# One decoder layer with three token mixers and 32 experts on one core: taps ahead of the search, Silu later, squares summed by TensorE, sums of a block together

## The chip, the cores and the metric

The kernel runs on one core of a Trainium2 chip. The core has TensorE (PE in the profile; PEld is its weight load), VectorE (DVE), ScalarE (ACT), GpSimd (POOL) and SyncE (SP, which issues the DMAs), each with its own queue of instructions, worked off in order. The metric is the device time of one execution in microseconds (us). An execution that was profiled also leaves a trace; its span is the time from the first to the last instruction.

## The reference, cut to what matters

One layer for 512 tokens of width 1024, in float32:

```python
h = rms_norm(x, n1g) * (1 + sc1) + sh1
qm, km, vm, ca, cg, qd, kd, vd, qi, ki, wi = split(h @ w_in)
y_moba = moba_attention(qm, km, vm)            # 6 heads
y_conv = silu(layer_norm(causal_conv31(ca * sigmoid(cg))))   # 256 channels
y_dsa  = dsa_attention(qd, kd, vd, qi, ki, wi) # 6 heads, the 128 best keys per query
mix = concat([rms_norm(y_moba, mg), y_conv, rms_norm(y_dsa, dg)])
x = x + g1 * (mix @ w_out)
h2 = rms_norm(x, n2g) * (1 + sc2) + sh2
y = hier_moe(h2)   # best of 4 groups, best 2 of its 8 experts, each (silu(x@w1) * (x@w3)) @ w2
return rms_norm(x + g2 * y, final_g)
```

The convolution has 31 taps per channel; each is one multiply-add over 512 tokens. The 128 best keys are found by 16 rounds, each of which takes the 8 largest scores of a row and strikes them out.

## The kernel before, in words

**Order.** Every engine executes in the order in which the Python program emits. The program is one walk along TensorE's projection: `h @ w_in`, unit after unit, 8 steps (k) to a unit, three matmuls to a step (L458 to L460 for values, L463 to L465 for the rest, since operands are split in a high and a low part). Around it everything else is woven in by three devices. `step()` is called after each k step: it runs what was put off with `after(n, f)` once n steps are over, and on every third step (TEVERY = 3) it emits one entry of the list `taps`. `spent(us)` is told how long TensorE will be busy, times a rate, and spends that credit on three background lists `bg`, the first list that isn't empty first: `bg[0]` (the norm of group m and sums for the conditioning), `bg[1]` (the rounds of the top-score search on VectorE, L686 and L689) and `bg[2]` (VectorE's part of the convolution).

**Attention.** An item is a group (m or d), a query tile of 128 and a pair of heads: score matmuls (L628, L630), mask and row maximum on VectorE (L824), exponential on ScalarE (L826), scaling on VectorE (L834) and GpSimd (L838), then after some steps transposes (L845), copies to SBUF on ScalarE (L847), then the product with the values (L859) and a copy (L864). Items of group d need the mask of the search. After the third pair of a tile, `f3` squares the result on ScalarE (L868), GpSimd adds the three squares (L870, twice), and `f4` sums over the partitions by a matmul with ones (L878) into one column of the bank `pss[m]`. Once a group of tiles (GROUPS: tile 0 and tiles 1 to 3 for d) is done, the inverse root is taken on VectorE (L253 to L258), spread by L330, and applied.

**Convolution.** It has two halves of 128 channels. Of 31 taps per half, VectorE does a first one (L708) and 16 more (L712), ScalarE and GpSimd do 14 as a chain: ScalarE multiplies into a buffer of pool `g`, of which there are two (L723), and GpSimd adds (L724); the first of the 14 needs no addition (L719, L720). At the end of VectorE's list, `f2` emits whatever is left in `taps` at once and joins both sums (L729). Three steps (L5 = 3) after the second half, `conv_norm` has TensorE sum the channels (L743), VectorE subtract the mean (L750), ScalarE square, GpSimd add (L754), TensorE sum (L760), then the inverse root, its spreading (L330), the multiplication (L768) and Silu (L769).

**Tail.** After the projection (`tail[0] = 1`) the program goes on stepping until all twelve pieces of the mix are there, and the output projection (L1066 to L1068) and the last attention items of group d share TensorE.

**Experts.** 16 blocks of slots follow, the first alone and most others in pairs. A block does up-products with w1 (`up1`, 32 matmuls of 64x512, L1484), with w3 (`up3`), a transposition (L1508) and down-products (L1518); w1, w3 and w2 come by DMA from SyncE's queue. The result of a block is added to the tokens one block later by `added(nh)`, for each half nh of the columns: 8 matmuls (L1544) into four banks and four VectorE additions (L1536). In the odd blocks 1 to 13 `added(0)` is called in the middle of `up1` and `added(1)` behind it, each once.

Of the kernel before, what the change touches and what calls it, by code (L numbers as in the profile page):

```python
# [13 lines left out]
OP = mybir.AluOpType  # L14
PSUM = bass.MemoryType.PSUM

P = 128
T = 512
NT = 4
D = 1024  # L20
KD = 8
# [52 lines left out]
GROUPS = {"m": ((0, 1, 2, 3),), "d": ((0,), (1, 2, 3))}  # L74
# [8 lines left out]
def tile_hybrid_layer(  # L83
# [75 lines left out]
    def ps(shape, dt=F32):  # L159
        return mk(pp, shape, dt, "ps", 8)  # L160
# [60 lines left out]
    def col(name, j=0, n=1):  # L221
        i, r = rows[name]
        return pcol[i][:, r + j:r + j + n]
# [37 lines left out]
    def rsqrt(r, v, n, shape, apart=True):  # L261
        for f in rsqrt_ops(r, v, n, [P, r.shape[1]], apart):
            f()
# [263 lines left out]
    def spent(us):  # L527

        credit[0] = min(credit[0] + us * rate[0], CRED)
        while any(bg):  # L530
            b = [b for b in bg if b][0]
            if credit[0] < b[0][0]:
                break
            d, f = b.pop(0)
            credit[0] -= d
            f()
# [9 lines left out]
    def after(n, f):  # L546
        later.append([n, f])
# [192 lines left out]
    def conv_norm():  # L740
        pmean = ps([P, T])
        for j in range(2):
            PE.matmul(pmean, ones, cy[j], start=j == 0, stop=j == 1)  # L743
        spent(1.7)
        st = {}

        def f1():
            sq = []
            for j in range(2):
                V.scalar_tensor_tensor(cy[j], pmean, -1.0 / 256, cy[j], op0=OP.mult, op1=OP.add)  # L750
                q = ta([P, T])
                A.activation(q, cy[j], AF.Square)
                sq.append(q)
            G.tensor_tensor(sq[0], sq[0], sq[1], op=OP.add)  # L754
            after(L4, lambda: f2(sq[0]))

        def f2(sq):
            pv = ps([P, NT])
            for t_ in range(NT):
                PE.matmul(pv[:, t_:t_ + 1], sq[:, t_ * P:(t_ + 1) * P], ones[:, 0:1], start=True, stop=True)  # L760
            r = mk(sm, [P, NT], F32, "r4", 3)
            rsqrt(r, pv, 256, [P, NT])
            after(4, lambda: f3(r))

        def f3(r):
            p = spread(r).rearrange("p t q -> p (t q)")
            for j in range(2):
                V.tensor_tensor(cy[j], cy[j], p, op=OP.mult)  # L768
                A.activation(cu[j], cy[j], AF.Silu, bias=col("lb", j), scale=col("lg", j))  # L769
            for t_ in range(NT):  # L770
                for j in range(2):
                    mixed.append((t_, 3 + j, 1, cu[j][:, None, t_ * P:(t_ + 1) * P]))
        after(2, f1)
# [33 lines left out]
    def lag(i):  # L807

        return LT[i] if tail[0] else (L1, L2, L3, L4)[i]

    def att_item(m, qt, j):
# [39 lines left out]
        def f3():  # L851
            if (m, 6 + j) not in qkv:
                after(1, f3)
                return
            y = ps([P, P])
            for kt in range(qt + 1):
                for e in range(2):
                    hp = slice(64 * e, 64 * e + 64)
                    PE.matmul(y[hp], qkv[m, 6 + j][:, kt, hp], pT[e][:, kt * P:(kt + 1) * P],  # L859
                              start=kt == 0, stop=kt == qt)  # L860
            spent(0.22 * (qt + 1))
            if (m, qt) not in ym:
                ym[m, qt] = tq([P, 3, P])
            A.copy(ym[m, qt][:, j], y)  # L864
            npair[m, qt] = npair.get((m, qt), 0) + 1
            if npair[m, qt] == 3:
                sq = ta([P, 3, P])
                A.activation(sq, ym[m, qt], AF.Square)  # L868
                for i in (1, 2):
                    G.tensor_tensor(sq[:, 0], sq[:, 0], sq[:, i], op=OP.add)  # L870
                after(lag(3), lambda: f4(sq))

        def f4(sq):
            if m not in pss:
                pss[m] = ps([P, NT])
            pv = pss[m][:, qt:qt + 1]
            done.setdefault(m, set()).add(qt)
            PE.matmul(pv, sq[:, 0], ones[:, 0:1], start=True, stop=True)  # L878
            for g in GROUPS[m]:
                if qt in g and done[m].issuperset(g):  # L880
                    r = mk(sm, [P, NT], F32, "r4", 3)[:, :len(g)]
                    rsqrt(r, pss[m][:, g[0]:g[-1] + 1], 384, [P, NT])
                    after(L6 + 3 * (m == "m"), lambda r=r, g=g: f5(r, g))

        def f5(r, tiles):
# [432 lines left out]
    class Block:  # L1318
# [165 lines left out]
                    PE.matmul(self.pu[s, :], self.feature(k)[:, s], self.w[i][e][k // 4][:, k % 4, :],  # L1484
                              start=k == 0, stop=k == KD - 1)

        def up1(self, also=lambda: None):
            n = self.n
            self.up(0, range(4))
            also()  # L1490
            self.up(0, range(4, KD))
            self.hs = ta([P, T])
            A.activation(self.hs[:n], self.pu[:n], AF.Silu)  # L1493

# [207 lines left out]
    def added(nh):  # L1702

        if nh in old:
            blk, y = old.pop(nh)
            blk.combine(nh, y)
# [26 lines left out]
    for b in range(NB):  # L1733
# [5 lines left out]
            nxt = None if last else pair.blks[1 - b % 2]  # L1739

        fill = b > 0 and (b % 2 == 0 or last)
        cur.up1(lambda: None if fill else added(0))
        if b == 0:
            for t_ in range(2, NT):
                for i in range(2):
# [191 lines left out]
```

## Time and profile before

| | us |
|---|---|
| runs shown, three | 842.48, 844.48, 844.45 |
| their median | 844.45 |
| profiled execution | 841.79 |
| its span | 840.0 |
| TensorE busy in it | 803.2 |
| VectorE busy | 440.1 |
| ScalarE busy | 268.6 |
| GpSimd busy | 266.5 |

The profile is of one execution. Its page gives busy times, the trace behind it each instruction with its start, its duration and what ended the idle time before it. A granted clock of 1.00 means 2.4 GHz on TensorE, 0.50 means 1.2 GHz. Matmuls overlap by a part of their length, so a row's start plus its duration can lie behind the next row's start.

### The profile page before, as it was taken

The page shows a single profiled execution, that of the slowest core. Times are in us where ns is not written, and L with a number is a line of the kernel's source. Part 1 is how long each engine was busy: PE and PEld are TensorE (multiplying, and loading weights), DVE is VectorE, ACT ScalarE, POOL GpSimd, SP SyncE. Part 2 cuts the span into 40 slices and gives each one's busy share as a digit, 9 for nine tenths or more (in the row PEclk, how much of TensorE's full clock was granted, in tenths as well). Part 3 has the DMA queues.
Part 4 walks back from the last instruction along what each step waited for, and adds up shares of the span by engine and source line. Part 5 has one row for each costly group of instructions (what it writes and reads, how often), then busy time and mean ns, then how long its engine had stood idle before and what let it go on. Part 6 is the DMA issues. An engine that isn't in the chain of part 4 may idle for free.

```text
span 840.0 us, 12498 instructions
## 1 busy us (share of the span) xinstructions
PE 803.2 (96%) x4669; PEld 478.7 (57%) x4669; DVE 440.1 (52%) x1053; ACT 268.6 (32%) x577; POOL 266.5 (32%) x318
## 2 busy tenths in 40 slices
PE   6999999999989899999999999999999999999992
PEld 4888786677756678445446346436436445454442
DVE  4768888998767556673253152342333232332334
ACT  5277677646557333431101011101001001101024
POOL 0464876765403560605023031050050050050032
PEclk9999999999999999999999999999999999999997
DMA  9980574174215557789799999999999999999932
GB/s 346 337 194 1 201 234 158 48 265 150 65 64 183 244 204 305 288 339 393 283 420 419 420 420 418 420 419 419 418 421 418 421 418 420 419 419 394 375 120 103
DMA packets 75657, 252.00 MB, mean 300 GB/s; under 512 B 7511, under 2 KB 40385, under 8 KB 50506
## 3 DMA queue, kind: packets, MB, share of 16 engines
q1 hardware_dynamic: 75530, 251.15, 77.3%
q8 instruction: 38, 0.62, 0.3%
q14 instruction: 25, 0.20, 0.1%
q10 hardware_dynamic: 64, 0.02, 0.0%
HBM read 249.05 MB, written 2.10 MB: 299 GB/s over the span
## 4 chain that ended last, share of the span: by engine, by line
PE 84%; DVE 6%; ACT 3%; POOL 2%; DMA 1%; issue 1%; SPq 1%; ACTq 0%; POOLq 0%; DVEq 0%
PE ps L1484 26%; PE ps L1518 13%; PE ps L1544 7%; PE ps L1580 6%; PE ps L463 4%; PE ps L465 3%; PE ps L464 3%; PE ps L458 2%; PE ps L974 2%; DMA ad<-in_ada_w_dram 1%; PE ps L459 1%; PE ps L460 1%; PE ps L859 1%; PE ps L845 1%; PE ps L1508 1%
## 5 line engine op out<-in xcount | busy, mean ns | idle before, releaser
L1564 POOL TENSOR_SCALAR v<-c,sm 128x128 bf16<-128x128 f32 x112 | 65.0, 602 | 308.9 <-DVE sm L1595 308.9
L1484 PE MATMUL ps<-u,x 128*64 128x512 f32 x280 | 103.2, 594 | 0.0
L341 POOL TENSOR_TENSOR u<-r,u 128x512 fp32r<-128x512 f32 x55 | 73.6, 1345 | 54.2 <-ACT u L340 43.3
L1536 DVE TENSOR_TENSOR q<-ps,q 128x512 f32<-128x512 f32 x116 | 71.3, 681 | 32.3 <-PE ps L1544 32.3
L1501 DVE SCALAR_TENSOR_TENSOR a<-a,sm,ps 128x512 f32<-128x512 f32 x16 | 12.0, 747 | 133.9 <-PE ps L1484 97.8
L1484 PE MATMUL ps<-h,x 128*64 128x512 f32 x248 | 78.9, 594 | 0.0
L1484 PE MATMUL ps<-r,x 128*64 128x512 f32 x240 | 77.9, 593 | 0.0
L1518 PE MATMUL ps<-u,a 128*64 128x512 f32 x200 | 68.4, 595 | 0.0
L1529 ACT CAST a<-ps 128x512 fp32r<-128x512 f32 (+1 forms) x33 | 18.9, 573 | 133.0 <-DVE ps L1528 133.0
L1528 DVE TENSOR_TENSOR ps<-ps,q 128x512 f32<-128x512 f32 (+1 forms) x33 | 22.4, 678 | 68.0 <-PE ps L1518 68.0
L1544 PE MATMUL ps<-a,v 128*128 128x512 f32 (+1 forms) x132 | 53.9, 410 | 0.0
L463 PE MATMUL ps<-h,u 128*128 128x512 f32 x128 | 53.7, 419 | 0.0
L1484 PEld LDWEIGHTS ps<-u,x 128*64 128x64 f32 x280 | 31.5, 137 | 37.8 <-issue 35.6
L1518 PE MATMUL ps<-h,a 128*64 128x512 f32 (+1 forms) x144 | 50.5, 572 | 0.6 <-DVE g L1531 0.6
L1544 PE MATMUL ps<-g,v 128*128 128x512 f32 (+1 forms) x132 | 50.7, 386 | 0.0
L465 PE MATMUL ps<-h,u 128*128 128x512 f32 x128 | 50.5, 395 | 0.0
L464 PE MATMUL ps<-h,u 128*128 128x512 f32 x128 | 50.4, 394 | 0.0
L1484 PEld LDWEIGHTS ps<-r,x 128*64 128x64 f32 x240 | 24.2, 137 | 38.4 <-issue 35.5
L1588 ACT ACTIVATE x<-ps,c,c 128x256 f32<-128x256 f32 x28 | 14.3, 560 | 90.5 <-PE ps L1580 90.5
L1518 PE MATMUL ps<-r,a 128*64 128x512 f32 x120 | 43.0, 596 | 0.0
L1484 PEld LDWEIGHTS ps<-h,x 128*64 128x64 f32 x248 | 24.2, 137 | 31.1 <-issue 29.9
L1493 ACT ACTIVATE a<-ps 128x512 f32<-128x512 f32 x16 | 9.6, 598 | 99.7 <-PE ps L1484 91.4
(379 smaller groups left out, 1805.3 us busy)
## 6 DMA issues: line engine op xcount, KB each, us to landing
u<-in_expert_w_dram SPq DMA_DIRECT2D x60, 1024.0 KB
r<-in_expert_w_dram SPq DMA_DIRECT2D x48, 1024.0 KB
h<-in_expert_w_dram SPq DMA_DIRECT2D x46, 1024.0 KB
z<-in_expert_w_dram SPq DMA_DIRECT2D x24, 1024.0 KB
r<-in_ada_w_dram SPq DMA_DIRECT2D x16, 1024.0 KB
r<-in_w_in_dram SPq DMA_DIRECT2D x22, 512.0 KB
ad<-in_ada_w_dram SPq DMA_DIRECT2D x8, 1024.0 KB
h<-in_expert_w_dram SPq DMA_DIRECT2D x16, 256.0 KB
```

The lines of the kernel that those rows point to most:

```text
L341: eng.tensor_tensor(l, r, h.bitcast(F32), op=OP.subtract)
L463: PE.matmul(p, wh, h, start=k == 0, stop=False)
L464: PE.matmul(p, wh, l, start=False, stop=False)
L465: PE.matmul(p, wl, h, start=False, stop=k == KD - 1)
L1484: PE.matmul(self.pu[s, :], self.feature(k)[:, s], self.w[i][e][k // 4][:, k % 4, :], start=k == 0, stop=k == KD - 1)
L1518: PE.matmul(self.py[nh][s, cs], self.hT[:, k, s], self.second(e, k, nh)[:, cs], start=k == 0, stop=k == 3)
L1528: V.tensor_tensor(y, y, g2b[nh][:n, cs], op=OP.mult)
L1529: A.copy(yh, y)
L1536: V.tensor_tensor(xr[t_, nh], self.product(yy, t_), xr[t_, nh], op=OP.add)
L1544: PE.matmul(pc[:, cs] if held else pc, self.ot[:n, t_ * P:(t_ + 1) * P], yy[q][:n, cs], start=not held and q == 0, stop=last and q == 1)
L1564: ops.append(lambda o=b.choice(ch, t_), c_=c_[:, t_:t_ + 1]: eng.tensor_scalar(o, iota, c_, None, op0=OP.is_equal))
L1580: PE.matmul(p[:, kk], hb[q][t_][i][:, k * P:k * P + P], self.o[t_ // 2][:, t_ % 2], start=t_ == 0 and q == 0, stop=t_ == NT - 1 and q == 1)
```

## The change

1. `spent` serves the lists in the order `bg[0]`, `bg[2]`, `bg[1]`: VectorE's taps come before the rounds of the search.
2. The two Silus and the entries into `mixed` become `f4` of the convolution's norm, five steps after the multiplications.
3. In the tail (the last four tiles of group d) GpSimd's two additions of squares are left out; TensorE accumulates the three parts by three matmuls instead of one, and this comes one step sooner.
4. Each group of tiles has a bank of its own for its sums (`pss[m, gi]`).
5. `up1` isn't divided any more; `added(0)` and `added(1)` follow each other behind it in the odd blocks.

```diff
--- before.py
+++ after.py
@@ -528,7 +528,8 @@
 
         credit[0] = min(credit[0] + us * rate[0], CRED)
         while any(bg):
-            b = [b for b in bg if b][0]
+
+            b = [b for b in (bg[0], bg[2], bg[1]) if b][0]
             if credit[0] < b[0][0]:
                 break
             d, f = b.pop(0)
@@ -766,6 +767,11 @@
             p = spread(r).rearrange("p t q -> p (t q)")
             for j in range(2):
                 V.tensor_tensor(cy[j], cy[j], p, op=OP.mult)
+
+            after(5, f4)
+
+        def f4():
+            for j in range(2):
                 A.activation(cu[j], cy[j], AF.Silu, bias=col("lb", j), scale=col("lg", j))
             for t_ in range(NT):
                 for j in range(2):
@@ -866,20 +872,25 @@
             if npair[m, qt] == 3:
                 sq = ta([P, 3, P])
                 A.activation(sq, ym[m, qt], AF.Square)
-                for i in (1, 2):
-                    G.tensor_tensor(sq[:, 0], sq[:, 0], sq[:, i], op=OP.add)
-                after(lag(3), lambda: f4(sq))
-
-        def f4(sq):
-            if m not in pss:
-                pss[m] = ps([P, NT])
-            pv = pss[m][:, qt:qt + 1]
+
+                direct = bool(tail[0])
+                if not direct:
+                    for i in (1, 2):
+                        G.tensor_tensor(sq[:, 0], sq[:, 0], sq[:, i], op=OP.add)
+                after(lag(3) - direct, lambda: f4(sq, direct))
+
+        def f4(sq, direct):
+            gi = [qt in g for g in GROUPS[m]].index(True)
+            if (m, gi) not in pss:
+                pss[m, gi] = ps([P, NT])
+            pv = pss[m, gi][:, qt:qt + 1]
             done.setdefault(m, set()).add(qt)
-            PE.matmul(pv, sq[:, 0], ones[:, 0:1], start=True, stop=True)
-            for g in GROUPS[m]:
+            for i in range(3 if direct else 1):
+                PE.matmul(pv, sq[:, i], ones[:, 0:1], start=i == 0, stop=i == 2 * direct)
+            for gi, g in enumerate(GROUPS[m]):
                 if qt in g and done[m].issuperset(g):
                     r = mk(sm, [P, NT], F32, "r4", 3)[:, :len(g)]
-                    rsqrt(r, pss[m][:, g[0]:g[-1] + 1], 384, [P, NT])
+                    rsqrt(r, pss[m, gi][:, g[0]:g[-1] + 1], 384, [P, NT])
                     after(L6 + 3 * (m == "m"), lambda r=r, g=g: f5(r, g))
 
         def f5(r, tiles):
@@ -1484,11 +1495,9 @@
                     PE.matmul(self.pu[s, :], self.feature(k)[:, s], self.w[i][e][k // 4][:, k % 4, :],
                               start=k == 0, stop=k == KD - 1)
 
-        def up1(self, also=lambda: None):
+        def up1(self):
             n = self.n
-            self.up(0, range(4))
-            also()
-            self.up(0, range(4, KD))
+            self.up(0)
             self.hs = ta([P, T])
             A.activation(self.hs[:n], self.pu[:n], AF.Silu)
 
@@ -1739,7 +1748,7 @@
             nxt = None if last else pair.blks[1 - b % 2]
 
         fill = b > 0 and (b % 2 == 0 or last)
-        cur.up1(lambda: None if fill else added(0))
+        cur.up1()
         if b == 0:
             for t_ in range(2, NT):
                 for i in range(2):
```

Line numbers of the changed program are higher by 1 from L531 on, by 6 from the Silu on, by 9 to 11 from `f4(sq, direct)` on.

On GpSimd, the taps of the second half in the program before; q is the sum of a half, g the product of ScalarE's tap, u a split weight, v a softmax part.

```order
L724 TENSOR_TENSOR q_1336<-q_1336,g_1604 128x505
L838 TENSOR_TENSOR v_1576<-v_1576,sm_296_1564 128x128
L341 TENSOR_TENSOR u_1587<-r_1205,u_1587 128x512
L724 TENSOR_TENSOR q_1336<-q_1336,g_1677 128x504
L838 TENSOR_TENSOR v_1653<-v_1653,sm_316_1641 128x256
L341 TENSOR_TENSOR u_1715<-r_1415,u_1715 128x512
L724 TENSOR_TENSOR q_1336<-q_1336,g_1741 128x503
L724 TENSOR_TENSOR q_1336<-q_1336,g_1760 128x502
L838 TENSOR_TENSOR v_1730<-v_1730,sm_336_1718 128x384
L341 TENSOR_TENSOR u_1715<-r_1415,u_1715 128x512
L724 TENSOR_TENSOR q_1336<-q_1336,g_1818 128x501
```

The same engine after the change, from the addition that stands ahead of the last seven taps of the second half.

```order
L844 TENSOR_TENSOR v_1407<-v_1407,sm_237_1395 128x384
L341 TENSOR_TENSOR u_1415<-r_1185,u_1415 128x512
L725 TENSOR_TENSOR q_1203<-q_1203,g_1481 128x504
L725 TENSOR_TENSOR q_1203<-q_1203,g_1487 128x503
L725 TENSOR_TENSOR q_1203<-q_1203,g_1490 128x502
L725 TENSOR_TENSOR q_1203<-q_1203,g_1493 128x501
L725 TENSOR_TENSOR q_1203<-q_1203,g_1496 128x500
L725 TENSOR_TENSOR q_1203<-q_1203,g_1499 128x499
L725 TENSOR_TENSOR q_1203<-q_1203,g_1502 128x498
L844 TENSOR_TENSOR v_1464<-v_1464,sm_253_1452 128x512
L341 TENSOR_TENSOR u_1572<-r_1185,u_1572 128x512
```

Before, an addition for a weight or a softmax part stood between most taps; now the seven from 504 to 498 columns follow one another, and the 512-column softmax part and the next weight stand behind them.

On TensorE, the two matmuls that sum the channels for the convolution's mean (L743, of the two halves q) in the program before.

```order
L460 MATMUL ps_2532<-u_2172,h_107 128x256
L458 MATMUL ps_2532<-u_2172,h_105 128x256
L459 MATMUL ps_2532<-u_2172,h_105 128x256
L460 MATMUL ps_2532<-u_2172,h_107 128x256
L878 MATMUL ps_2347<-c_94,a_2403 128x1
L743 MATMUL ps_2606<-q_1913,c_94 128x512
L743 MATMUL ps_2606<-q_2235,c_94 128x512
L458 MATMUL ps_2532<-u_2172,h_105 128x256
L459 MATMUL ps_2532<-u_2172,h_105 128x256
```

The same two (now L744) after the change, with what stands around them.

```order
L629 MATMUL ps_1546<-q_1113,q_1111 128x256
L629 MATMUL ps_1547<-q_1114,q_1112 128x256
L631 MATMUL ps_1546<-q_1178,q_1111 128x256
L631 MATMUL ps_1547<-q_1178,q_1112 128x256
L463 MATMUL ps_1516<-h_105,u_1296 128x512
L464 MATMUL ps_1516<-h_107,u_1296 128x512
L465 MATMUL ps_1516<-h_105,u_1296 128x512
L744 MATMUL ps_1564<-q_924,c_94 128x512
L744 MATMUL ps_1564<-q_1195,c_94 128x512
L463 MATMUL ps_1516<-h_105,u_1296 128x512
L464 MATMUL ps_1516<-h_107,u_1296 128x512
```

Before, they stood among the projection of values, far behind the taps; now they stand in the projection of an earlier unit, one step behind the score matmuls of an attention item (L629, L631).

On TensorE, the middle of `up1` in an odd block before (L1484 up, L1544 sums of the block in front).

```order
L1484 MATMUL ps_4570<-r_4435,x_4254 64x512
L1484 MATMUL ps_4570<-u_4437,x_4254 64x512
L1544 MATMUL ps_4579<-a_4530,v_4354 128x512
L1544 MATMUL ps_4579<-g_4531,v_4354 128x512
L1544 MATMUL ps_4583<-a_4530,v_4354 128x512
L1544 MATMUL ps_4583<-g_4531,v_4354 128x512
L1544 MATMUL ps_4587<-a_4530,v_4354 128x512
L1544 MATMUL ps_4587<-g_4531,v_4354 128x512
L1544 MATMUL ps_4591<-a_4530,v_4354 128x512
L1544 MATMUL ps_4591<-g_4531,v_4354 128x512
L1484 MATMUL ps_4570<-u_4439,x_4254 64x512
L1484 MATMUL ps_4570<-u_4441,x_4254 64x512
```

The same block after the change, from the end of `up1`.

```order
L1495 MATMUL ps_4571<-u_4440,x_4255 64x512
L1495 MATMUL ps_4571<-u_4442,x_4255 64x512
L1495 MATMUL ps_4571<-u_4440,x_4255 64x512
L1495 MATMUL ps_4571<-u_4442,x_4255 64x512
L1553 MATMUL ps_4614<-a_4531,v_4355 128x512
L1553 MATMUL ps_4614<-g_4532,v_4355 128x512
L1553 MATMUL ps_4618<-a_4531,v_4355 128x512
L1553 MATMUL ps_4618<-g_4532,v_4355 128x512
```

The eight matmuls of `added(0)` went from the middle of the 32 up-products to behind them.

## Rows read from the trace of the kernel before

**Rows 1.** The page's first part: busy us, share of the span, instructions.

```profile
PE 803.2 (96%) x4669; PEld 478.7 (57%) x4669; DVE 440.1 (52%) x1053; ACT 268.6 (32%) x577; POOL 266.5 (32%) x318
```

**Rows 2.** Stretches: length, busy us by engine, granted clock, DMA share, GB/s.

```profile
120.00:140.00 20.00, 20.00 (x123) 13.36 (x121) 18.72 (x48) 14.47 (x38) 14.42 (x13) 1.00 0.52 159
247.00:290.00 43.00, 34.36 (x209) 23.56 (x208) 29.27 (x84) 25.96 (x65) 18.09 (x22) 0.96 0.55 208
252.70:256.05 3.35, 3.35 (x15) 2.80 (x13) 2.82 (x8) 2.21 (x5) 0.00 (x0) 0.50 0.52 149
444.58:504.40 59.82, 59.82 (x323) 29.07 (x324) 20.20 (x37) 6.76 (x12) 11.30 (x18) 1.00 1.01 420
804.00:808.00 4.00, 4.00 (x19) 2.06 (x15) 1.71 (x3) 0.00 (x0) 1.56 (x2) 1.00 0.39 125
```

**Rows 3.** TensorE's waits, 246 to 292 us: for whom, total, times, longest.

```profile
PE ps L859 <- ACT a L847: 5.5, 2, 4.2
PE ps L878 <- POOL a L870: 1.3, 2, 0.8
PE ps L330 <- DVE r L258: 1.0, 2, 0.8
PE ps L878 <- DVE ps L253: 0.9, 1, 0.9
```

**Rows 4.** The chain of waits from 425 to 510 us: start, duration, what.

```profile
433.49 3.43 PE ps L1484 x16
436.93 2.04 PE ps L1544 x8
438.96 3.58 PE ps L1484 x16
...
468.20 13.73 PE ps L1484 x64
...
484.45 1.85 PE ps L1544 x8
```

**Rows 5.** TensorE's timeline: start, duration, what; in brackets idle before, releaser.

```profile
133.59 0.39 PE L465 MATMUL ps<-h,u 128*128 128x512 f32 x1
...
220.27 1.96 PE L743 MATMUL ps<-q,c 128*128 128x512 f32 x4
...
237.58 0.94 PE L760 MATMUL ps<-c,a 128*128 128x1 f32 x8
...
251.66 1.37 PE L859 MATMUL ps<-a,q 128*64 128x128 f32 x12 [4.19 <-ACT a L847]
```

**Rows 6.** ScalarE's timeline from 246 to 251 us.

```profile
247.06 1.28 ACT L769 ACT_TABLE_LOAD   x1
249.42 1.52 ACT L769 ACTIVATE q<-q,m 128x512 f32<-128x512 f32 x2 [1.08 <-DVE q L768]
```

**Rows 7.** GpSimd's taps by line: count, ns of shortest, median, longest.

```profile
L724 POOL TENSOR_TENSOR q<-q,g x26: 1257/1276/1422, 80.8 to 168.1; 128x510 f32<-128x510 f32 x2, 128x509 f32<-128x509 f32 x2, 128x508 f32<-128x508 f32 x2, 128x507 f32<-128x507 f32 x2
```

**Rows 8.** GpSimd's timeline, three places between 130 and 194 us.

```profile
130.00 1.29 POOL L341 TENSOR_TENSOR u<-r,u 128x512 fp32r<-128x512 f32 x1 [1.27 <-ACT u L340]
131.26 1.27 POOL L724 TENSOR_TENSOR q<-q,g 128x507 f32<-128x507 f32 x1
134.84 1.27 POOL L838 TENSOR_TENSOR v<-v,sm 128x512 f32<-128x512 f32 x1 [2.32 <-DVE sm L830]
...
192.48 1.44 POOL L341 TENSOR_TENSOR u<-r,u 128x512 fp32r<-128x512 f32 x1 [1.76 <-ACT u L340]
```

**Rows 9.** VectorE's timeline, two places.

```profile
130.71 0.68 DVE L689 MATCH_REPLACE8 b<-sm,b 128x512 f32<-128x512 f32 x1
...
191.62 0.69 DVE L729 TENSOR_TENSOR q<-q,q 128x512 f32<-128x512 f32 x1
...
192.81 1.63 DVE L712 SCALAR_TENSOR_TENSOR q<-q,m,q 128x482 f32<-128x482 f32 x1
```

**Rows 10.** VectorE's taps by line: count, ns of shortest, median, longest.

```profile
L712 DVE SCALAR_TENSOR_TENSOR q<-q,m,q x32: 719/772/1819, 168.8 to 218.0; 128x482 f32<-128x482 f32 x2, 128x483 f32<-128x483 f32 x2, 128x484 f32<-128x484 f32 x2, 128x485 f32<-128x485 f32 x2
```

## The prediction

> **What bounds the kernel now.** I read the busy times first. TensorE is busy 803.2 of 840.0 us [rows 1], so the time can only move where TensorE idles or where its own matmuls get shorter or more. Next, by stretches [rows 2]: between 120 and 140 us TensorE is busy throughout, and VectorE beside it 18.72 of 20 us, with GpSimd at 14.42; between 247 and 290 us TensorE works 34.36 of 43 us, which leaves 8.64 idle; in a pair of expert blocks (444.58 to 504.40) it has no gap at all. A fifth row shows the granted clock at 0.50 from 252.70 to 256.05, that is at 1.2 GHz. So there are three stages with different laws: attention and projection, where TensorE is full but VectorE nearly so; the tail, where TensorE waits; and the experts, where only the length of the matmuls counts. The waits of the tail name whom TensorE waits for: 5.5 us for ScalarE's copies, 1.3 for GpSimd, 1.0 and 0.9 for VectorE [rows 3].
>
> The profiled execution took 841.79 us (span 840.0 and 1.79 around it); the median of the runs shown is 844.45, so 2.66 above it. I sum against the profiled execution and put the difference onto 844.45.
>
> **Both sums of the block in front together.** In an odd block, TensorE now goes from 16 up-products to 8 products of the earlier block, back to 16, and again to 8. The chain shows it: 3.43, 2.04, 3.58, 2.04, then 32 for the second up matrix; until there 11.09 us [rows 4] (the 2.04 stands twice in a block). Where 64 up-products run unbroken they take 13.73, so 32 take 6.87; and where 8 products follow 8 others, with four short transposes between, they take 1.85 [rows 4]. The new order costs 6.87 + 2.04 + 1.85 = 10.76, which is 0.33 less. Seven blocks (1, 3, ... 13) have it: 2.3 us. What could eat it: the 8 results per group go to VectorE and need eight buffers; 16 in a row ask for twice that, but the 32 matmuls behind them (6.87 us by the same row) don't depend on the additions. I put that at nothing; without that cover it costs at most the 0.33 again. The upper end is 0.33 + 0.19 (if both groups took 1.85) = 0.52 a block, 3.6 us. Taken: -2.3, from 0 to -3.6.
>
> **The tail.** TensorE's longest wait there is 4.19 us, up to 251.66, for a copy of ScalarE [rows 3, 5]. ScalarE was not slow at copying; before the copy it loaded the table for Silu (1.28), waited 1.08 for VectorE's product and ran two Silus (1.52), from 247.06 to 250.94 [rows 6]. With the convolution gone from there, all of that leaves: 1.28 + 1.08 + 1.52 = 3.9 of the 4.19. Behind that idle stretch the granted clock stood at 0.50 for 3.35 us [rows 2]; work done there at full rate would have taken half, so 1.7 more go with it. The second wait on that copy is 5.5 - 4.2 = 1.3 us, where no Silu stands ahead; I count half, 0.6 (0 to 1.3). The sums of squares: waits of 1.3 for GpSimd's additions (they fall out for the last four tiles of group d) and 0.9 because a matmul shared a bank with a sum that VectorE was reading [rows 3]; both go, 2.2. Late next is ScalarE's square itself, and I take it that the matmul, which now comes one step sooner, just meets it. The price is eight more matmuls on TensorE: eight records, four such matmuls, took 0.94 [rows 5], so 0.235 each, 1.9 us; below, nothing, if they fill idle time. Sum: -3.9 - 1.7 - 0.6 - 2.2 + 1.9 = -6.5, from -4 to -10.3 (the whole idle time and the 1.7). The Silu moved into the dense stretch brings its two table loads along; it comes five steps behind the product, so the 1.08 is not waited for again, and TensorE has projection steps to run meanwhile; 0 to 2.6 us, I take 0.
>
> **The taps ahead of the search.** This is the dear part. VectorE's 16 taps of each half now run early, before the rounds of the top-score search, but the 14 taps that ScalarE and GpSimd share still come one per three steps. When VectorE's list reaches its end, all that remain are issued at once. The order shows it for the second half: GpSimd has seven taps (504 to 498 columns) without a break, and TensorE's two matmuls for the mean stand only one projection step behind an attention item that the trace shows near 133 us. Each such tap costs GpSimd 1.276 us in the median [rows 7]. They start once GpSimd has finished the addition at 130.00 to 131.29, which stands just ahead of the seven now; before, it stood ahead of the tap of 507 columns alone [rows 8]. So the seven end at 131.3 + 7 x 1.276 = 140.2; VectorE's joining addition takes 0.69 [rows 9]; the matmul can start at 140.9. TensorE would reach it at 133.59 + 0.39 = 134.0, does the first half's matmuls (half of 1.96) until 135.0, and waits 5.9 us [rows 5]. Nothing in that queue can pass: behind it stand the projection's matmuls and all attention. An idle stretch that long is longer than the one near 250, so I charge the same half rate behind it: 1.7.
>
> Behind the burst follow smaller debts. VectorE stood still from about 133 to 140 at the joining addition, on an engine with 1.3 us free in 20 [rows 2], so its next softmax parts come late. GpSimd's 512-column addition, 1.27 us [rows 8], stands behind the seven taps, and the transposes wait for it; ScalarE's copies stand behind its own taps, since there are only two tap buffers. I bound this by nothing (TensorE runs slower there anyway and leaves time) and by 5 (VectorE's lost time paid once more), and take 1.3, that one addition.
>
> Last, VectorE and GpSimd beside each other. The trace has a tap on VectorE from 192.81 that took 1.63 us while GpSimd added from 192.48 to 193.92 [rows 8, 9], against 0.719 for the shortest of 32 [rows 10]. A search round beside a GpSimd tap is not stretched: 0.68 at 130.71 and the GpSimd tap beside it 1.27 [rows 8, 9]. Now VectorE's taps meet both GpSimd's taps and its additions; in return the slow ones around 190 us go. If 14 taps ahead of the burst were all held for 0.9, that were 12.6 us of VectorE, of which the joining wait hides about half: +6. If none, 0; and the lighter stretch later may give back 1: -1. The median of the 32 is 0.772, near the low end, so I take +1.
>
> The Trainium skill ("SBUF — State Buffer", section "Who interferes with whom") states that a VectorE instruction with two SBUF inputs contends with a GpSimd instruction that reads SBUF, and that the later one blocks fully. The tap at 192.81, which ends where the addition's end plus one tap would put it (193.92 + 0.72 = 194.64, read 194.44), agrees. By that rule taken for every tap the upper end of +6 would hold and the total would be 5 us higher; it is the second rival below.
>
> Part sum: 5.9 + 1.7 + 1.3 + 1 = +9.9, from +5 (the bare stall less 1) to +18.6.
>
> **Total.** -2.3 - 6.5 + 9.9 = +1.1 us: 842.9 against the profiled execution, 845.6 against the median.
>
> **Rivals.**
> - *The tail was held by the convolution alone.* Then all 8.64 us of its idle time and the 1.7 go and the eight matmuls fall into gaps, -10.3; with -2.3 and a stall of 5.9 + 1.7 + 1.3: -3.7, so 840.7. For it: the tail's first and longest wait is that one copy, and all later ones lie behind it. Against it: TensorE's waits for the inverse root on VectorE (1.0 us in two [rows 3]) stay in the change. It decides where the tail returns over 10 us.
> - *VectorE and GpSimd hold each other throughout.* The other side: the upper end of the last term, +6 in place of +1: +6.1, so 850.6; up to 854.3 with the debts at 5. It decides where VectorE's taps ahead of the burst average over 1.3 us. For it: the tap at 192.81. Against: the median of 0.772.
> - *The experts are bound by their weights.* The DMA share in a pair is 1.01 at 420 GB/s [rows 2]; if TensorE got faster than the weights, the 2.3 would come back as waits: +3.4, so 847.9. Against: near the end (804 to 808) the share is only 0.39, so the last weights were in well ahead of use, and seven times 0.33 us fits into such a lead.
>
> **How the numbers follow.** Under 0.3% (2.5 us) no change can be told. Forecast 0.43 (same 0.26, slower 0.13, faster 0.04); tail rival 0.33 (faster 0.31, same 0.02); mutual holding 0.16, slower; weights 0.08 (slower 0.06, same 0.02). So faster 0.35, same 0.30, slower 0.35. The range reaches from the tail rival with the experts at their upper end and half a stall (840.7 - 1.3 - 3 = 836.4) to mutual holding with its debts (854.3); the forecast's own is 841 to 850.
>
> **What would show it.** TensorE's matmuls for the mean with a wait of about 6 us on VectorE's joining addition near 135 to 141 us, and seven GpSimd taps in a row ahead of it; no wait of 4 us near 250, no Silu there, and no wait of a sum of squares on GpSimd; odd blocks 0.33 us shorter with no wait on a DMA. I am wrong if the mean's matmuls don't wait, if the tail's waits only change their name, or if VectorE's taps before 135 us take well over 0.8 us in the median.

## The result and the profile after

The changed kernel takes 856.34 us in the median of three runs (853.31 to 856.45), against 844.45: the ratio is 1.0132, interval 1.0113 to 1.0150. That is 11.9 us slower, beyond the upper end of the range (854.3) and on the side of the second rival. The profiled execution took 853.31 us with a span of 851.5, so its span is 11.5 above the one of before; the terms below are summed against that.

The page's first part, to be read beside [rows 1]: TensorE is busy 3.8 us longer, so most of the loss is idle time.

```profile
PE 807.0 (95%) x4685; PEld 484.1 (57%) x4685; DVE 447.8 (53%) x1053; ACT 268.8 (32%) x577; POOL 267.5 (31%) x310
```

The stretches after, columns as in [rows 2].

```profile
120.00:140.00 20.00, 13.66 (x61) 8.85 (x60) 19.58 (x34) 9.22 (x27) 14.05 (x11) 0.83 0.38 107
128.10:133.20 5.10, 5.10 (x13) 3.62 (x14) 4.99 (x12) 4.52 (x14) 3.27 (x3) 0.50 0.00 2
140.00:160.00 20.00, 12.13 (x59) 7.61 (x58) 9.05 (x27) 10.13 (x22) 12.50 (x10) 0.74 0.14 52
152.00:157.00 5.00, 5.00 (x8) 2.60 (x9) 4.42 (x15) 0.81 (x3) 1.32 (x2) 0.50 0.00 0
258.00:300.00 42.00, 40.29 (x270) 28.51 (x270) 29.67 (x82) 29.50 (x79) 12.30 (x13) 1.00 0.52 194
447.25:506.69 59.44, 59.44 (x322) 29.25 (x320) 20.11 (x37) 6.76 (x12) 11.63 (x18) 1.00 1.01 419
```

Between 120 and 140 us, where TensorE had been busy throughout [rows 2], it now works 13.66 of 20 us, and 12.13 in the 20 us after, and the granted clock stands at 0.50 in two stretches of 5.10 and 5.00 us, each behind a long wait. VectorE is full in the first half (19.58 of 20) and mostly idle in the second (9.05). The tail, now at 258 to 300 us, idles 1.71 us where it idled 8.64, and at full clock throughout. A pair of expert blocks takes 59.44 instead of 59.82.

TensorE's waits from 80 to 180 us (for whom, total, times, longest):

```profile
PE ps L744 <- ACT q L870: 7.9, 1, 7.9
PE ps L851 <- DVE v L840: 4.8, 1, 4.8
PE ps L851 <- POOL v L844: 1.5, 1, 1.5
```

Its timeline at these places:

```profile
126.19 0.30 PE L851 MATMUL ps<-c,v 128*128 128x128 f32 x1 [4.82 <-DVE v L840]
128.02 0.47 PE L851 MATMUL ps<-c,v 128*128 128x128 f32 x1 [1.52 <-POOL v L844]
...
143.63 0.39 PE L465 MATMUL ps<-h,u 128*128 128x512 f32 x1
151.89 3.78 PE L744 MATMUL ps<-q,c 128*128 128x512 f32 x4 [7.87 <-ACT q L870]
...
185.84 0.63 PE L851 MATMUL ps<-c,v 128*128 128x128 f32 x4 [2.93 <-DVE v L840]
```

The last projection matmul ahead of the mean starts at 143.63; before, the same one started at 133.59 [rows 5]. So it comes 10.0 us later, ahead of the wait that the prediction had named, and that wait then took 7.87. Neither 4.82 nor 1.52 stands in the sum of the prediction. But 0.9 of the 10.0 isn't theirs: the first projection matmul (L463) already starts at 50.47 instead of 49.58. The granted clock was 0.50 from 13.9 to 17.2 us, and 1.00 there before. Nothing that the change moves runs so early, and over the twelve runs of the layer that start lies between 49.5 and 51.6. So 9.1 us fall to what the change did.

The wait of 2.93 at 185.84, and one of 0.18 for GpSimd right behind it, are for a softmax part that was waited for in the kernel before too:

```profile
160.76 0.66 PE L845 MATMUL ps<-c,v 128*128 128x128 f32 x4 [1.76 <-DVE v L834]
```

There they were 1.76 and 0.24, so 1.1 us are new. VectorE's two multiplications of the convolution's norm (L769, 1.28 us from 182.69) now stand in its queue ahead of that part.

The starts of the same matmuls in both traces give the loss by stages:

| us from the span's start | before | after | the stage up to there |
|---|---|---|---|
| first projection matmul (L463) | 49.58 | 50.47 | +0.9 |
| the projection matmul ahead of the tail (L463) | 244.45 | 266.86 | +21.5 |
| first up-product of the experts (L1484, now L1495) | 344.52 | 358.59 | -8.3 |
| end of the span | 840.0 | 851.5 | -2.6 |

VectorE's taps, grouped by line, against [rows 10]:

```profile
L713 DVE SCALAR_TENSOR_TENSOR q<-q,m,q x32: 715/1464/1819, 81.3 to 141.1; 128x482 f32<-128x482 f32 x2, 128x483 f32<-128x483 f32 x2, 128x484 f32<-128x484 f32 x2, 128x485 f32<-128x485 f32 x2
```

The median went from 0.772 to 1.464 us. GpSimd's taps, against [rows 7], went from 1.276 to 1.460:

```profile
L725 POOL TENSOR_TENSOR q<-q,g x26: 1234/1460/1768, 81.7 to 151.1; 128x510 f32<-128x510 f32 x2, 128x509 f32<-128x509 f32 x2, 128x508 f32<-128x508 f32 x2, 128x507 f32<-128x507 f32 x2
```

VectorE's timeline: four taps on end, a scaling of a softmax part, and the joining addition.

```profile
118.08 4.80 DVE L713 SCALAR_TENSOR_TENSOR q<-q,m,q 128x482 f32<-128x482 f32 x4
...
124.92 1.12 DVE L840 TENSOR_SCALAR v<-v,sm 128x128 f32<-128x128 f32 x1
...
152.41 0.69 DVE L730 TENSOR_TENSOR q<-q,q 128x512 f32<-128x512 f32 x1 [10.56 <-POOL q L725]
```

Four taps take 4.80, and the scaling of a 128x128 part, which starts at 124.92 and whose shortest in the whole trace is 0.285, takes 1.12; it is what TensorE waits 4.82 us for. GpSimd's timeline:

```profile
137.29 1.69 POOL L725 TENSOR_TENSOR q<-q,g 128x505 f32<-128x505 f32 x1
...
141.95 1.28 POOL L341 TENSOR_TENSOR u<-r,u 128x512 fp32r<-128x512 f32 x1 [2.07 <-ACT u L340]
143.19 9.18 POOL L725 TENSOR_TENSOR q<-q,g 128x504 f32<-128x504 f32 x7
```

A tap beside VectorE's work takes 1.69; the seven of the burst, while VectorE stands at the joining addition, take 9.18, or 1.31 each. ScalarE's timeline, the end of its part of the burst:

```profile
149.78 0.71 ACT L724 ACTIVATE g<-q,m 128x498 f32<-128x498 f32 x1 [0.61 <-POOL q L725]
...
151.57 0.27 ACT L870 COPY q<-ps 128x128 f32<-128x128 f32 x1
```

This corrects a detail of the mean's wait. TensorE is released at 151.89, when ScalarE's copy L870 (151.57 and 0.27) is done, which stands behind ScalarE's seven taps, the last five of which wait for GpSimd to free one of two buffers. The reason is a bank: in the program as built, that copy reads a result of attention out of the bank that the mean's sum is then written to. The mean's first matmul waits for this copy alone, the second for the joining addition, which ends 1.2 us after, while the first half's matmuls run.

### The profile page after: what moved, and what is told of

Same layout as the page of the kernel before. It is cut to its first block, busy times and chain, and to the rows that moved or that the text cites. A ratio compares the mean times of both kernels' runs of the same rounds, so it can differ in the third digit from the quotient of the medians.

```text
span 851.5 us, 12532 instructions
## 1 busy us (share of the span) xinstructions
PE 807.0 (95%) x4685; PEld 484.1 (57%) x4685; DVE 447.8 (53%) x1053; ACT 268.8 (32%) x577; POOL 267.5 (31%) x310
## 4 chain that ended last, share of the span: by engine, by line
PE 80%; DVE 11%; issue 3%; POOL 2%; ACT 2%; DMA 1%; SPq 0%; ACTq 0%; POOLq 0%; DVEq 0%
PE ps L1495 26%; PE ps L1527 12%; PE ps L1553 7%; PE ps L1589 6%; DVE q L713 3%; PE ps L463 2%; PE ps L465 2%; PE ps L464 2%; PE ps L865 1%; PE ps L384 1%; PE ps L458 1%; PE ps L985 1%; PE ps L851 1%; PE ps L418 1%; PE ps L420 1%
## 5 line engine op out<-in xcount | busy, mean ns | idle before, releaser
L1495 PE MATMUL ps<-u,x 128*64 128x512 f32 x280 | 102.7, 593 | 0.0
L1495 PE MATMUL ps<-h,x 128*64 128x512 f32 x248 | 78.7, 593 | 0.0
L1495 PE MATMUL ps<-r,x 128*64 128x512 f32 x240 | 77.6, 593 | 0.0
L463 PE MATMUL ps<-h,u 128*128 128x512 f32 x128 | 55.6, 434 | 0.0
L1495 PEld LDWEIGHTS ps<-u,x 128*64 128x64 f32 x280 | 31.8, 137 | 38.6 <-issue 37.1
L464 PE MATMUL ps<-h,u 128*128 128x512 f32 x128 | 51.2, 400 | 0.0
L465 PE MATMUL ps<-h,u 128*128 128x512 f32 x128 | 51.1, 399 | 0.0
L1495 PEld LDWEIGHTS ps<-r,x 128*64 128x64 f32 x240 | 24.4, 137 | 38.6 <-issue 36.8
L1495 PEld LDWEIGHTS ps<-h,x 128*64 128x64 f32 x248 | 24.3, 137 | 31.3 <-issue 28.8
L832 ACT ACTIVATE v<-v,sm 128x128 f32<-128x128 f32 (+3 forms) x48 | 26.6, 556 | 46.7 <-DVE sm L830 46.5
```

The costliest lines, as they stand in the source:

```text
L463: PE.matmul(p, wh, h, start=k == 0, stop=False)
L464: PE.matmul(p, wh, l, start=False, stop=False)
L465: PE.matmul(p, wl, h, start=False, stop=k == KD - 1)
L832: A.activation(s[e][:, :n], s[e][:, :n], AF.Exp, bias=rm, scale=-1.0, accum_out=rs[:, e:e + 1])
```

## The experiments

Two theories from the start. **Theory 1**: part 1 carries the whole loss, by two causes, the burst of seven GpSimd taps at the end and the mutual holding of VectorE's taps and GpSimd's instructions. The rivals take one of the two alone, or blame the Silu or the parts together.

### Each part alone

Part 1 alone, on the kernel before:

```diff
-            b = [b for b in bg if b][0]
+            b = [b for b in (bg[0], bg[2], bg[1]) if b][0]
```

> The kernel before with part 1 alone: VectorE's taps ahead of the search. Theory 1 (this part carries the whole loss; the other parts only gain): the attention stage loses some 20 us against the kernel before, as in the changed kernel, and the tail gets the 4.2 us wait and the half rate behind it back: about +14 us, ratio 1.014 to 1.020, slower than the changed kernel. Rival (the loss comes from the Silu put later, or from the parts together): ratio within 1.000 to 1.008.

Measured: 1.0205 (1.0188 to 1.0222), 860.74 us. Its waits from 80 to 180 us are those of the changed kernel:

```profile
PE ps L743 <- ACT q L864: 7.9, 1, 7.9
PE ps L845 <- DVE v L834: 4.8, 1, 4.8
PE ps L845 <- POOL v L838: 1.4, 1, 1.4
```

So the loss comes with part 1; the other parts gain on top. The ratio is just above what was expected (1.014 to 1.020), and one expectation failed: the wait of 4.2 us near 250 does not come back. It is part 1 that takes the convolution out of the tail. Up to the tail this run loses 22.1 us, and the tail (the third row of the table) gives 5.1 back. The Silu's wait has only moved: TensorE waits 3.55 us for ScalarE's copy at 185.63, behind the table load and the Silus.

All parts but the first, the changed kernel with the old line of `spent`:

```diff
-            b = [b for b in (bg[0], bg[2], bg[1]) if b][0]
+            b = [b for b in bg if b][0]
```

> The changed kernel without part 1: the search ahead of the taps as before, parts 2 to 5 kept. Theory 1: no long wait at the mean's matmuls, no late softmax parts; about 2.3 us gained in the experts and 0 to 2 in the tail, ratio 0.994 to 0.998. Rival (Silu five steps later delays the start of the output projection when the convolution is last): the tail loses 2 to 4 us, ratio 0.998 to 1.002. If the loss lay in parts 2 to 5: ratio over 1.008.

Measured: 0.9967 (0.9953 to 0.9980), 841.26 us. From 80 to 246 us TensorE waits for one softmax part, 1.8 us, as in the kernel before. But the tail shows the rival at work. TensorE's timeline there:

```profile
247.71 1.25 PE L865 MATMUL ps<-a,q 128*64 128x128 f32 x12 [0.29 <-ACT a L853]
250.67 1.07 PE L851 MATMUL ps<-c,v 128*128 128x128 f32 x8 [1.71 <-DVE v L840]
...
255.91 0.67 PE L1077 MATMUL ps<-u,h 128*128 128x512 f32 x1 [3.48 <-DVE h L801]
```

The wait for the copy fell from 4.19 [rows 5] to 0.29, and two others came, 1.71 and 3.48. The convolution's entries come into `mixed` five steps later, and a token tile of the mix is split (L801), as the output projection (L1077) needs it, only once all its entries are there: so the split stands later in VectorE's queue, behind work of attention.

Part 5 alone, on the kernel before:

```diff
         def up1(self):
-            self.up(0, range(4))
-            also()
-            self.up(0, range(4, KD))
+            self.up(0)
...
-        cur.up1(lambda: None if fill else added(0))
+        cur.up1()
```

> The kernel before with part 5 alone: both sums of the block in front together. Theory: 0.33 to 0.38 us per odd block, seven blocks, 2.3 to 2.7 us less, ratio 0.997. Rival (the weights' DMAs bound the experts): waits on DMA in the experts, ratio 1.000.

Measured: 0.9968 (0.9954 to 0.9982), 841.34 us, with no wait on a DMA in the experts. The changed kernel's chain shows the new order (start, duration, what), against [rows 4]:

```profile
447.25 6.87 PE ps L1495 x32
454.11 3.85 PE ps L1553 x16
```

6.87 and 3.85 in place of 3.43 + 2.04 + 3.58 + 2.04 is 0.37 less, seven times 2.6 us.

Parts 3 and 4 alone, on the kernel before:

```diff
+                direct = bool(tail[0])
+                if not direct:
+                    for i in (1, 2):
+                        G.tensor_tensor(sq[:, 0], sq[:, 0], sq[:, i], op=OP.add)
+                after(lag(3) - direct, lambda: f4(sq, direct))
...
+            if (m, gi) not in pss:
+                pss[m, gi] = ps([P, NT])
```

> The kernel before with parts 3 and 4 alone: TensorE adds the last squares, a bank for each group of tiles. Theory: 2.2 us of waits leave the tail, 1.9 us of matmuls come: -0.3 us, ratio 0.9985 to 1.0005. Rival (GpSimd's additions held the chain to the tail's end): 2 to 4 us less, ratio 0.995 to 0.998.

Measured: 0.9963 (0.9951 to 0.9976), 841.03 us. That is the rival's size: 3.1 us, not 0.3. TensorE's waits from 246 to 310 us, against [rows 3]:

```profile
PE ps L862 <- ACT a L850: 5.5, 2, 4.2
...
PE ps L330 <- DVE r L258: 0.2, 1, 0.2
```

Both waits of L878 are gone and of the 1.0 for the inverse root 0.2 is left. That makes 3.0. The tail (245.00 to 342.76, before 244.45 to 344.52) is 2.3 us shorter in this trace, so less than the 1.9 reckoned for the eight matmuls shows as a cost.

### What in part 1 costs

VectorE's taps left out of the changed kernel:

```diff
         def f1(w):
             s = 30 - w
-            V.scalar_tensor_tensor(cy[j][:, s:], cu[j][:, :T - s], col("cw", 2 * w + j), cy[j][:, s:], ...)
```

> The changed kernel with VectorE's 32 multiply-adds of the convolution left out; its first tap, the joining additions and all of GpSimd's taps stay. Theory 1 (two causes: VectorE's taps and GpSimd hold each other, which makes the softmax parts late, and the burst of seven GpSimd taps by itself): GpSimd's taps fall from 1.46 to 1.28 us in the median, the waits of the transposes on VectorE and GpSimd (4.8 and 1.5) go, but the matmuls of the mean still wait 5 to 7 us for the burst, with half rate behind: about 11 us less than the changed kernel, ratio to the kernel before 1.000 to 1.004. Rival A (the mutual holding alone; the burst is only late because of it): the mean's wait goes too, ratio 0.985 to 0.992. Rival B (the burst alone): little changes, ratio 1.009 to 1.014.

Measured: 1.0016 (1.0005 to 1.0027), 845.38 us: 0.0116 under the changed kernel's ratio, or 10 us. GpSimd's taps and the mean's matmuls:

```profile
L723 POOL TENSOR_TENSOR q<-q,g x26: 1232/1270/1474, 80.8 to 139.5; 128x510 f32<-128x510 f32 x2, 128x509 f32<-128x509 f32 x2, 128x508 f32<-128x508 f32 x2, 128x507 f32<-128x507 f32 x2
```

```profile
140.28 3.78 PE L742 MATMUL ps<-q,c 128*128 128x512 f32 x4 [5.95 <-ACT q L868]
```

GpSimd's median is back at 1.270, the waits for softmax parts ahead of the mean are gone (TensorE reaches it 0.35 us later than before, 133.94 against 133.59), and the burst alone makes TensorE wait 5.95 us. Both causes are real, and rivals A and B fall. A wait of 2.96 for the later softmax part, at 174.21, stays.

GpSimd's taps left out of the changed kernel:

```diff
                 A.activation(t[:, s:], cu[j][:, :T - s], AF.Copy, scale=col("cw", 2 * w + j))
-                G.tensor_tensor(cz[j][:, s:], cz[j][:, s:], t[:, s:], op=OP.add)
```

> The changed kernel with GpSimd's 26 additions of the convolution left out; ScalarE's multiplications and VectorE's taps stay. Theory 1: no burst; VectorE's taps fall from 1.46 to near 0.8 us in the median (weights' additions on GpSimd still hold some), and all three long waits go: about 20 us less than the changed kernel, ratio to the kernel before 0.987 to 0.994. Rival C (VectorE is late because of the number of its taps, not because GpSimd holds them): the wait of 4.8 us for the softmax part stays, ratio 0.998 to 1.006.

Measured: 0.9937 (0.9914 to 0.9960), 837.89 us: 0.0195 under the changed kernel's ratio, or 16 us. VectorE's taps and the mean's matmuls:

```profile
L713 DVE SCALAR_TENSOR_TENSOR q<-q,m,q x32: 712/730/1818, 81.3 to 130.8; 128x482 f32<-128x482 f32 x2, 128x483 f32<-128x483 f32 x2, 128x484 f32<-128x484 f32 x2, 128x485 f32<-128x485 f32 x2
```

```profile
137.26 3.47 PE L743 MATMUL ps<-q,c 128*128 128x512 f32 x4 [2.37 <-ACT q L869]
```

With as many VectorE taps in the same order the median is 0.730, and the wait of 4.8 is gone. So VectorE was not late by the number of its taps (rival C); it was held. That all three long waits go, as had been expected, did not come about: what is left of the mean's, 2.37, stands behind ScalarE's seven multiplications, and the later softmax part is waited for 2.50 us.

The mean nine steps later:

```diff
-L5 = 3
+L5 = 12
```

> The changed kernel with the norm of the convolution 12 steps behind the taps instead of 3 (L5). Theory 1: the mean's wait (7.9 us and half rate behind) is covered by nine steps of projection and the attention between; the earlier waits for the softmax parts stay: 7 to 10 us less than the changed kernel, ratio to the kernel before 1.002 to 1.006. Rival D (the mean's wait is only the first to meet the burst; the transposes behind GpSimd's 512-column addition and the copies behind ScalarE's taps wait as long): ratio over 1.009.

Measured: 1.0108 (1.0091 to 1.0126), 853.71 us. The gain of 7 to 10 us did not come, only 2, and the interval overlaps that of the changed kernel; this is rival D. TensorE's timeline:

```profile
153.47 1.93 PE L865 MATMUL ps<-a,q 128*64 128x128 f32 x12 [6.25 <-ACT a L853]
157.77 1.94 PE L851 MATMUL ps<-c,v 128*128 128x128 f32 x8 [2.37 <-DVE v L840]
```

The same burst now holds the copies (6.25) and then a softmax part (2.37): whatever stands first behind ScalarE's taps waits for it.

A tap every second step, so that no burst is left:

```diff
-TEVERY = 3
+TEVERY = 2
```

> The changed kernel with a GpSimd tap every second step in place of every third (TEVERY), so that no tap is left for a burst at the end of either half. Theory 1 (burst and holding are two causes): the mean's wait of 7.9 us falls under 3, but VectorE meets a busier GpSimd, so its taps stay at 1.4 us or more and the transposes wait 6 us or more for the softmax parts: 4 to 8 us less than the changed kernel, ratio to the kernel before 1.004 to 1.010. Rival A (the holding alone): no change or slower, ratio over 1.012. Rival B (the burst alone): all of the 20 us in that stage come back, ratio under 0.996.

Measured: 1.0078 (1.0062 to 1.0095), 850.95 us: 0.0054 under the changed kernel's ratio, or 4.6 us. VectorE's taps, and TensorE's waits from 80 to 180 us:

```profile
L713 DVE SCALAR_TENSOR_TENSOR q<-q,m,q x32: 711/1572/1739, 82.7 to 147.0; 128x482 f32<-128x482 f32 x2, 128x483 f32<-128x483 f32 x2, 128x484 f32<-128x484 f32 x2, 128x485 f32<-128x485 f32 x2
```

```profile
PE ps L851 <- DVE v L840: 4.9, 2, 4.4
PE ps L985 <- DMA r<-in_ada_w_dram: 3.1, 1, 3.1
PE ps L851 <- POOL v L844: 3.0, 1, 3.0
...
PE ps L744 <- DVE q L730: 0.2, 1, 0.2
```

The mean waits 0.2 us, as it should without a burst. But the taps take 1.572 in the median, the softmax parts cost 7.9 us of waits, and a new wait came, 3.1 for a DMA of the conditioning's weights. Spreading the taps removed one cause and fed the other.

The Silu where it was, with the taps first:

```diff
-            after(5, f4)
-        def f4():
             for j in range(2):
                 A.activation(cu[j], cy[j], AF.Silu, ...)
```

> The changed kernel without part 2: the Silus right behind the multiplications. Theory: with the taps first, the Silu stands in the dense stretch near 180 us, where ScalarE's queue would wait 1 us for VectorE's product: 0.5 to 1.5 us slower than the changed kernel, ratio to the kernel before 1.013 to 1.017. Rival (the place makes no difference there): as the changed kernel, within 0.002 of it.

Measured: 1.0127 (1.0107 to 1.0147), 855.03 us, the same as the changed kernel. Part 2 makes no difference in time there, as its rival said. In the trace one wait takes the place of another: TensorE waits 3.56 us at 185.40 for a copy behind the Silu, where the changed kernel waits 2.93 and 0.18 for the softmax part. With the taps behind the search part 2 costs something (above).

### The holding by itself

Seven stretches, eight instructions of 128x512 each, in float32, in a program that computes nothing of the layer and was executed once:

```diff
+    for _ in range(8):   # 3: both engines, all operands in SBUF
+        V.scalar_tensor_tensor(acc, src, one[:, 0:1], acc, op0=OP.mult, op1=OP.add)
+        G.tensor_tensor(gac, gac, gsr, op=OP.add)
+    for _ in range(8):   # 4: one of VectorE's operands in PSUM
+        V.scalar_tensor_tensor(acc, pin, one[:, 0:1], acc, op0=OP.mult, op1=OP.add)
+        G.tensor_tensor(gac, gac, gsr, op=OP.add)
```

> Seven stretches by themselves instead of the layer (none of the layer is computed): eight VectorE multiply-adds of 128x512 alone; eight GpSimd additions alone; both together; both with one of VectorE's inputs in PSUM; VectorE with one SBUF input beside the additions; the maximum of a search round beside them; the multiply-adds beside GpSimd only writing. Theory 1 (whole instructions hold each other where VectorE reads two operands from SBUF and GpSimd reads SBUF): 0.72 and 1.28 us alone, about 2.0 us for each pair together (the two add up, so VectorE's tap shows up to 1.8), and 0.72 and 1.28 again in stretches 4, 5, 6 and 7. Rival (both only share a bandwidth): each is some 30% longer in all stretches that read SBUF, and PSUM as a source changes nothing much.

VectorE's timeline. L73: multiply-adds alone; L83: beside GpSimd's additions; L89: the same with one operand in PSUM; L95: one SBUF operand and constants, L101: search maximum, both beside the additions; L108: multiply-adds beside GpSimd writing only. L59 is one instruction like L95, alone.

```profile
9.71 0.42 DVE L59 TENSOR_SCALAR k<-k 128x512 f32<-128x512 f32 x1
...
10.98 6.26 DVE L73 SCALAR_TENSOR_TENSOR k<-k,k 128x512 f32<-128x512 f32 x8
...
30.12 12.41 DVE L83 SCALAR_TENSOR_TENSOR k<-k,k 128x512 f32<-128x512 f32 x8
...
44.76 6.25 DVE L89 SCALAR_TENSOR_TENSOR k<-k,k 128x512 f32<-128x512 f32 x8
...
56.73 10.23 DVE L95 TENSOR_SCALAR k<-k 128x512 f32<-128x512 f32 x8
...
69.17 5.79 DVE L101 MAX8 k<-k 128x8 f32<-128x512 f32 x8
...
81.50 6.26 DVE L108 SCALAR_TENSOR_TENSOR k<-k,k 128x512 f32<-128x512 f32 x8
```

GpSimd's timeline: alone, beside L83, beside L89.

```profile
18.38 10.64 POOL L78 TENSOR_TENSOR k<-k,k 128x512 f32<-128x512 f32 x8 [17.94 <-DVE k L65]
30.35 13.30 POOL L84 TENSOR_TENSOR k<-k,k 128x512 f32<-128x512 f32 x8 [1.34 <-DVE k L65]
44.98 10.65 POOL L90 TENSOR_TENSOR k<-k,k 128x512 f32<-128x512 f32 x8 [1.33 <-DVE k L65]
```

Together a multiply-add goes from 0.78 to 1.55 us (an eighth of each row) and an addition from 1.33 to 1.66. With one operand in PSUM nothing happens to either (6.25, 10.65), nor to a multiply-add beside a GpSimd that only writes (6.26). The maximum takes 0.72 beside the additions; it wasn't run alone here, but took 0.69 in the kernel before. So it is not a shared bandwidth, which would have stretched all that read SBUF. But a pair takes 1.66, not the 2.11 of both alone: some 0.45 us of each pair overlap, and "about 2.0" was too much. Stretch 5 was also expected wrong: the one-operand instruction goes from 0.42 to 1.28, while the additions beside it take 1.39. The softmax scaling is close to that form (its factor is a column in SBUF, not a constant), so the likely reason for the 1.12 at 124.92 above is the same: in the changed kernel the scaling of a 128x384 part took 1.23 beside GpSimd, at 137.97, and 0.42 at 176.56.

The Trainium skill ("SBUF — State Buffer", section "Who interferes with whom") names both forms: two operands in SBUF against a reading GpSimd, and `tensor_scalar` when it uses both ports. The runs agree on who is held and who isn't. Its "fully blocks" would give the 2.11 us of both alone, and a pair took 1.66.

### The version that beats both

Parts 3, 4 and 5 on the kernel before, without parts 1 and 2:

```diff
+                direct = bool(tail[0])
...
+            self.up(0)
...
+        cur.up1()
```

> The kernel before with parts 3, 4 and 5: squares added by TensorE in banks of their own and both sums together, neither the taps first nor the Silu later. Theory: the gains of the two single runs add, -2.7 and -3.1 us: ratio 0.992 to 0.9945, the fastest so far. Rival (the tail and the experts share what is gained, or the weights' DMAs give the limit): ratio 0.995 to 0.997, as each alone.

Measured: 0.9939 (0.9922 to 0.9955), 839.19 us. The gains add. Against all parts but the first (0.9967) the later Silu costs about 2 us when the taps come last. The two intervals overlap a little, but the traces say the same: the tail takes 97.81 us here (247.10 to 344.91) and 100.36 there (244.40 to 344.76).

## Why the prediction was wrong

- **The step that failed** is in the taps: "The median of the 32 is 0.772, near the low end, so I take +1." The term measured 9.1 us ahead of the mean: 4.82 and 1.52 of waits and 5.10 us at half rate, which cost 2.6, so 8.9 of it. Even the end taken as worst, +6, was too small, so the second rival, which had the mechanism, was too cheap as well. With this term the part sum, +9.9 with +18.6 as its upper end, became 21.5. The prediction's own sign of being wrong came in: the 28 taps before 135 us took 1.54 in the median.
- Why it failed can be read in rows that stood there. GpSimd's last tap starts at 168.1 [rows 7], 1.26 us long, and VectorE's first at 168.8 [rows 10]: in the kernel before the two chains met for 0.6 us. While VectorE's taps ran there, from 168.75 to 218.70, GpSimd was busy 27.56 of 49.95 us with other work. A median over taps beside a half idle GpSimd says little on taps that run beside a full one. A tap that met an addition from end to end, 1.63 at 192.81 [rows 9], was the row to go by.
- The bound was also put on the wrong things. It counted only the taps ahead of the burst and hid half of them behind the joining wait. What mattered was that VectorE's queue, held twice as long per tap, delivers the softmax parts late; and that the scaling itself is held.
- **The burst** was right as a mechanism, and its length was: seven taps, 8.93 us from 131.29 predicted, 9.17 from 131.59 measured without VectorE's taps. That the wait agrees, 5.9 against 5.95, is partly luck. The prediction lets the first half's matmuls run and ends the wait of the second with VectorE's joining addition; measured, the first half's matmuls wait already, and ScalarE's copy releases them. In the changed kernel the wait is 7.87. The half rate behind it was charged at 1.7 and measured 5.00 us at 0.50, so 2.5.
- The smaller debts behind the burst, 1.3: the 1.1 us at the later softmax part, 3.1 in place of 2.0, but behind the norm's multiplications on VectorE and not behind GpSimd's addition.
- **The tail**: -6.5 predicted, -8.3 measured. Idle time fell by 6.9 (8.64 to 1.71) and the 1.7 of half rate went, together 8.6, so of the 1.9 charged for the matmuls little shows. The tail rival, which asked for over 10, falls. Inside the term the squares were undersized, 0.3 against 3.1 measured alone: the wait for the inverse root, said to stay, mostly went, and the matmuls cost less.
- **Both sums together**: -2.3 predicted, -2.6 to -2.7 measured; no weights were waited for, so the third rival falls. The working had a slip that cost nothing: eight products make four results in four banks, not eight.
- **The Silu later** at nothing: right in time with the taps first, where a wait for the softmax part takes the place of one for ScalarE's copy.
- The sum with measured terms: 0.9 (the start) + 9.1 + 7.9 + 2.5 + 1.1 - 8.3 - 2.6 = 10.6, of 11.5.

What stays open: the 0.9 us that this leaves, all of it ahead of the tail (20.6 of 21.5 are placed), and the size of what the later Silu costs with the taps last.

## What to carry to other kernels

Two chains of work on VectorE and GpSimd that read SBUF can hold each other when they meet (VectorE's multiply-adds took twice their time here); before moving one, look in the trace whether they have ever met, and price the move with the rows where they have. Work that is handed out by steps and "the rest at once" piles up where its consumer is moved forward: count what is left at that point, and look at every engine that the pile passes through (here ScalarE's copies). A change of five parts is worth taking apart: here one part cost 17 us and three others together gained 5.

## What the runs showed of the hardware

- A VectorE multiply-add with both operands in SBUF takes 1.55 us beside GpSimd additions and 0.78 alone; with one operand in PSUM it takes 0.78 beside them. The additions take 1.66 beside the former, 1.33 alone and beside the latter.
- A VectorE instruction with a single SBUF operand and constants in float32, 128x512, took 1.28 us beside them and 0.42 alone; the search's maximum took 0.72 beside them and 0.69 in the kernel before.
- The granted clock stood at 0.50 for about 5 us behind the waits of 7.87 us and of 4.82 and 1.52 us, and for 3.35 us [rows 2] behind one of 4.19. What follows a shorter wait wasn't fixed: behind 1.76 and 0.24 us for the same softmax part it stayed at 1.00 in the kernel before (162.5 to 166.5) and stood at 0.50 in the run of parts 3, 4 and 5 (163.7 to 167.0, behind 1.77 and 0.24).
